# Attention and chunk scores of a hybrid encoder trunk: two heads in step on the two halves of the array

## The chip, the core and the metric

The kernel runs on one core of one Trainium2 chip. The metric is the device time of one execution in microseconds (us). The kernel before takes 2495.84 us, the median of three runs (2495.49 to 2499.09). All products of this kernel run on the tensor engine (PE); VectorE is DVE, ScalarE is ACT, GpSimd is POOL, and SP issues the transfers.

## What is computed

Two layers of an encoder trunk over 512 tokens of 1024 channels, in fp32. Each layer has a half-step feed-forward part, one projection into three mixers that run side by side, an output projection, cross attention to 256 memory tokens, and a second feed-forward part. The change touches two of the mixers, each of six heads of 64 channels:

```python
# B: chunked attention; with 512 tokens every earlier chunk is in the band
s = einsum('bnihd,bnjhd->bhnij', qc, kb) * HEAD_DIM ** -0.5
prob = softmax(where(valid, s + bias, NEG_INF), axis=-1)
o = einsum('bhnij,bnjhd->bnihd', prob, vb)
# A: RWKV-7 recurrence, one step a token
sa = einsum('bhvk,bhk->bhv', S, -kk_t)
S = S * w_t + sa * (kk_t * a_t) + v_t * k_t
y = einsum('bhvk,bhk->bhv', S, r_t)
```

The recurrence is computed by chunks of 64 tokens. Each chunk needs masked products of decayed keys with decayed queries (its scores), the inverse of a triangular system, and a step of the state.

## The kernel before, in words

`trunk` runs `ffn`, `mixer`, `cross`, `ffn` for each layer. Dense products split weights and activations into a high and a low part and multiply three times (`mm3`, L155). All matmuls go through the helper `mm` (L78), elementwise DVE work through `tt` (L69) and `stt` (L72), ACT work through `act` (L75). An fp32 product with fp32 operands shows in the trace as two MATMULs (two passes); a transpose or a product of high and low parts as one.

The change lies in `mixer`, in its second part, where three generators run beside each other. `recurrence` (L618) walks through `systems`, `keyrows` and `chains` and sets the pace: for each of its steps, `dense` (projections of q, k, v and the pool) and `attention` get credit for a fraction of a step (ATT_RATE is 0.65). A `yield` ends a step. On top of that a scheduler orders each engine's instructions when the program is built, so the order on PE is fixed before the run. `dense` makes q and k of two heads a time (`unit`, tiles pqk, pqt); after each of the three units `attend` works on these two heads.

- `attend` (L657) takes the heads of a pair one after the other. A head's q and k lie on one half of the 128 partitions (rows 0 to 63 or 64 to 127). For four blocks of 128 queries: a score product into tile pbs (64 rows of the array, 128, 256, 384 or 512 columns streamed), the bias from tile toe added (tile e, L670), the maximum (L672), the exponential with its sum, a reciprocal (L674), and the scaling (L675). Then ten transposes (pbt, L683), four copies to ptb, and four products with V into tile pbo (64 columns of the array, streams of 512 to 128). Score and transpose tiles share the two PSUM banks "sm". There are 6 heads in each of 2 layers: 48 score products and 48 products with V.
- `systems` (L455) makes the scores of a chunk (tile psc): for head set g of two (row half g of the array), three products of 128 streamed columns, then the masks. Eight chunks a layer, six products each: 96 products.
- `chain` (L530) steps the state: tiles pr, pu, pst, py, with rhs and vu as copies between them, and a group norm at the end of each pair of chunks (pyt).
- After the generators, the output projection (pout, L780 to L790) multiplies first what the attention (mbhi, mblo) and the pool (mchi, mclo) gave, and last what the recurrence gave (mahi, malo).

Tiles ptt and pf are the doubling steps of `systems`, pgate and ppool the gate and the pool, pin, pqk and pbvf dense projections, ptr transposed keys.

Of the kernel before, what the change touches and what calls it, by code (L numbers as in the profile page):

```python
# [8 lines left out]
F32 = mybir.dt.float32  # L9
# [5 lines left out]
P = 128  # L15
T = 512
# [37 lines left out]
def trunk(tc, I, out, depth=DEPTH):  # L54
    nc = tc.nc
    ctx = ExitStack()
    with ctx:
# [73 lines left out]
        ones = const.tile([P, P], F32, name="ones")  # L131
# [42 lines left out]
        def proj_tok_steps(banks, ap, acts):  # L174
            """banks[i][128 tokens, 2, 256] = act[tokens]^T W, for W = ap [128, 8, 256]."""
            w = []
            for k0 in (0, 4):
                w += weights(ap[:, k0:k0 + 4].rearrange("p k m -> p (k m)"), 1024)
                for k in range(k0, k0 + 4):
                    s = slice(k % 2 * 256, k % 2 * 256 + 256)  # L180
                    wh, wl = w[k // 2]
                    ah, al = acts[k]
                    for b, p in enumerate(banks):
                        for i in range(2):
                            c = slice((2 * b + i) * P, (2 * b + i + 1) * P)
                            st = k == 0 and i == 0
                            mm(p[:, i], ah[:, c], wh[:, s], st, False)
                            mm(p[:, i], al[:, c], wh[:, s], False, False)
                            mm(p[:, i], ah[:, c], wl[:, s], False, k == 7 and i == 1)
                    yield  # L190
# [24 lines left out]
        def update(k, p, scale=None, spill=False, fetch=None):  # L215
            """x += scale * p; x leaves for DRAM or is fetched from there around the mixers."""
            if fetch is not None:
                x[k] = fetch
                nc.sync.dma_start(out=x[k], in_=x_dram[k])
            if scale is None:  # L220
                tt(x[k], x[k], p, add)
            else:
                stt(x[k], p, scale, x[k], mult, add)
            if spill:
                nc.sync.dma_start(out=x_dram[k], in_=x[k])
            square_in(k)

        def tok_rstd(sq, n, o, scale, e, tag="sm"):
            """o[128 tokens, n / 128] = 1/sqrt(scale * sum over channels of sq + e)."""
            p = bank(tag, "ptok")  # L230
            for i in range(n // P):
                mm(p[:, i:i + 1], sq[:, i * P:(i + 1) * P], ones[:, 0:1])
            act(o, p[:, :n // P], AF.Sqrt, bias=e, scale=scale)
            nc.vector.reciprocal(out=o, in_=o)

        def rstd(bcast=True, tag="sm"):
            """1/rms of x for each token, with the tokens on the rows and, on request, on the columns."""
            rt = tp.tile([P, 4], F32, tag="rtok", name="rtok", bufs=1)
            tok_rstd(ssq["a"], T, rt, 1.0, eps, tag)
            r = None  # L240
            if bcast:
                p = bank(tag, "psn")
                for i in range(4):
                    mm(p[:, i * P:(i + 1) * P], rt[:, i:i + 1].to_broadcast([P, P]), ident)
                r = tp.tile([P, T], F32, tag="rstd", name="rstd", bufs=1)
                act(r, p, AF.Copy)
            return r, rt
# [46 lines left out]
        def mixer(l):  # L294
# [4 lines left out]
            with mx as mp:  # L299
# [30 lines left out]
                # values  # L330
# [29 lines left out]
                # the low-rank inputs  # L360
# [6 lines left out]
                # while x is in DRAM its eight slots hold scratch of the preparation and then q and k of the attention  # L367
                # (later its output) and the biases
# [65 lines left out]
                # RWKV-7 by chunks of 64, two at a time  # L434
# [20 lines left out]
                def systems(q, o):  # L455
                    """For the pairs 2q and 2q + 1 of chunks, in two sets of heads g, g + 2, g + 4: the masked
                    scores and the inverse of each chunk's triangular system."""
                    nn = mp.tile([P, 2, 3, 2, HD], F32, tag="nn", name="nn", bufs=1)
                    ata, at = [], []
                    for c4 in range(4):  # L460
                        c, c2 = 4 * q + c4, c4 % 2
                        m = mp.tile([P, 3, 2, HD], F32, tag="ata", name="ata", bufs=6)
                        mr = mp.tile([P, 3, 2, HD], F32, tag="atr", name="atr", bufs=6)
                        for g in range(2):
                            s = bank("iv", "psc")[:, :AW].rearrange("p (j t) -> p j t", j=3)
                            for j in range(3):
                                mm(s[:, j], cols(kb, j, c)[halves[g]], cols(ar, j, c)[halves[g]])
                            tt(m[:, :, g], s[:, :, :HD], bc(C("mask")[:, :HD], 3), mult)
                            tt(mr[:, :, g], s[:, :, HD:], bc(C("mask")[:, HD:], 3), mult)
                        u = halves[1 - c2]  # L470
                        act(nn[u, c4 // 2], m[u], AF.Copy)
                        ata.append([m[:, :, g] for g in range(2)])
                        at.append([mr[:, :, g] for g in range(2)])
                        yield
                    # doubling the blocks of b: sources in the even blocks, targets in the odd ones. F holds no more
                    # than its blocks, so that the products need a mask only for which blocks pair up; and until
                    # the last step its 32-blocks hold all of it
# [33 lines left out]
                def keyrows(p):  # L511
                    """Keys on the rows, decayed to the chunk's end."""
# [17 lines left out]
                def chain(p):  # L530
                    """The state through chunks 2p and 2p + 1, and what they put out."""
                    ata, at, F, tr = sys[p]["ata"], sys[p]["at"], sys[p]["F"], trs[p]
                    y = mp.tile([P, 6, HD], F32, tag="y", name="y", bufs=2)
# [42 lines left out]
                    # group norm, bonus, gate  # L576
# [79 lines left out]
                # attention over all earlier chunks and the own one  # L656
                def attend(j, bq, bk, bvt):  # L657
                    po = bank("po", "pbo")
                    for hh in range(2):
                        hr = halves[hh]  # L660
                        toe = toes[hh]
                        nc.sync.dma_start(out=toe, in_=I["toep"][l, 2 * j + hh])
                        nc.gpsimd.memset(toe[0:64, T - HD:], -1e30)
                        prs = []
                        for qi in range(4):
                            n = (qi + 1) * P
                            s = sm("pbs")
                            mm(s[:, :n], bq[hr, qi * P:(qi + 1) * P], bk[hr, :n])
                            e = b2("e")
                            tt(e[:, :n], s[:, :n], toe[:, T - n:], add)  # L670
# [5 lines left out]
                            prs.append(e)  # L676
                            yield
                        pts = []
                        for ki in range(4):
                            n = (4 - ki) * P  # L680
                            pt = sm("pbt")
                            for qi in range(ki, 4):
                                nc.tensor.transpose(pt[:, (qi - ki) * P:(qi - ki + 1) * P], prs[qi][:, ki * P:(ki + 1) * P], ident)  # L683
                            q = mp.tile([P, n], F32, tag=f"ptb{ki}", name="ptb", bufs=1)
                            if ki % 2:
                                nc.vector.tensor_copy(out=q, in_=pt[:, :n])
                            else:
                                act(q, pt[:, :n], AF.Copy)
                            pts.append(q)
                        yield  # L690
                        for ki in range(4):
                            mm(po[hr, ki * P:], bvt[ki][:, (2 * j + hh) * HD:(2 * j + hh + 1) * HD], pts[ki], ki == 0, ki == 3)
# [3 lines left out]
                def pool():  # L696
                    # trailing windows: sums by doubling
                    pwt = mp.tile([P, 2, P], F32, tag="pwt", name="pwt")
                    nc.sync.dma_start(out=pwt, in_=I["poolw"][l])
                    for j in range(2):  # L700
                        def trail(o, i, n):
                            """o = i + i from n tokens before."""
# [58 lines left out]
                # the recurrence sets the pace; the dense products and the attention take steps at these rates beside it  # L761
# [32 lines left out]
        def cross(l):  # L794
            with tc.tile_pool(name=f"cx{l}", bufs=1) as cp:
# [26 lines left out]
                def head(w, acts, n, r, gain, tag, o, b):  # L822
                    """An RMS-normed head; the step it leaves behind puts the channels on the partitions, as high and low parts."""
# [159 lines left out]
def _pack(w, n=P):  # L983
    """[K, M] -> [M / n, 128, K / 128, n]: one contiguous run a partition for each tile of M."""
# [87 lines left out]
```

## Time and profile before

| what | value |
|---|---|
| median of three runs | 2495.84 us (2495.49 to 2499.09) |
| span of the profiled execution, the only time the page gives of it | 2493.6 us, 2.2 us below the median |
| PE busy | 2460.9 us, 99% of the span, 14058 MATMULs |
| DVE, ACT, POOL busy | 1300.3 us, 1007.5 us, 184.9 us |
| granted TensorE clock | 1.00 in every window read |
| second part of the mixer, layer 0 | 478 to 652 us, then the output projection to about 710 |
| the same of layer 1 | 1720 to 1893 us |

The page gives busy time for each engine, the chain of work that ended last, and groups of instructions; the timeline gives starts and lengths. Matmuls are pipelined: the length of one holds its way through the array, so that what a product costs PE is read from the start of one to the start of the next.

### The profile page before, as it was taken

The page shows a single profiled execution, that of the slowest core. Times are in us where ns is not written, and L with a number is a line of the kernel's source. Part 1 is how long each engine was busy: PE and PEld are TensorE (multiplying, and loading weights), DVE is VectorE, ACT ScalarE, POOL GpSimd, SP SyncE. Part 2 cuts the span into 40 slices and gives each one's busy share as a digit, 9 for nine tenths or more (in the row PEclk, how much of TensorE's full clock was granted, in tenths as well). Part 3 has the DMA queues.
Part 4 walks back from the last instruction along what each step waited for, and adds up shares of the span by engine and source line. Part 5 has one row for each costly group of instructions (what it writes and reads, how often), then busy time and mean ns, then how long its engine had stood idle before and what let it go on. Part 6 is the DMA issues. An engine that isn't in the chain of part 4 may idle for free.

```text
span 2493.6 us, 35631 instructions
## 1 busy us (share of the span) xinstructions
PE 2460.9 (99%) x14058; PEld 2001.1 (80%) x14058; DVE 1300.3 (52%) x2361; ACT 1007.5 (40%) x1804; POOL 184.9 (7%) x246
## 2 busy tenths in 40 slices
PE   8999999999999999999999999999999999999999
PEld 6888887877689888888888888867776898888887
DVE  5444335757575644443344443367676756444422
ACT  4333334434465543333333333343344655433322
POOL 1000002101020000000000000021111201000000
PEclk9999999999999999999999999999999999999999
DMA  3223333210242222323332233322102422222332
GB/s 134 95 99 94 106 114 102 69 45 20 68 143 99 71 93 94 102 93 93 93 99 96 95 98 110 119 72 68 45 25 70 148 88 71 94 100 94 99 110 87
DMA packets 72504, 225.27 MB, mean 90 GB/s; under 512 B 8177, under 2 KB 13201, under 8 KB 72337
## 3 DMA queue, kind: packets, MB, share of 16 engines
q1 hardware_dynamic: 72336, 223.00, 27.5%
q8 instruction: 110, 1.80, 0.3%
q14 instruction: 58, 0.47, 0.1%
HBM read 215.89 MB, written 7.08 MB: 89 GB/s over the span
## 4 chain that ended last, share of the span: by engine, by line
PE 95%; DVE 2%; issue 1%; ACT 1%; DMA 1%; POOL 0%; POOLq 0%; ACTq 0%; DVEq 0%; SPq 0%
PE po L78 20%; PE pu L78 20%; PE pg L78 19%; PE pxq L78 5%; PE pin L78 4%; PE pxw L78 3%; PE pqk L78 3%; PE pout L78 3%; PE pxv L78 2%; PE pbs L78 1%; PE pbvf L78 1%; PE pf L78 1%; PE ptt L78 1%; PE pbo L78 1%; PE pr L78 1%; PE psc L78 1%
## 5 line engine op out<-in xcount | busy, mean ns | idle before, releaser
L75 ACT ACTIVATE whi<-raw 128x512 fp32r<-128x512 f32 (+1 forms) x806 | 493.8, 614 | 964.9 <-PE po L78 323.9
L69 DVE TENSOR_TENSOR wlo<-raw,whi 128x512 fp32r<-128x512 f32 (+1 forms) x806 | 550.5, 685 | 570.4 <-ACT whi L75 566.7
L78 PE MATMUL pg<-hhi,whi 128*128 128x512 f32 x704 | 275.4, 391 | 6.6 <-ACT whi L75 6.6
L78 PE MATMUL po<-fhi,whi 128*128 128x512 f32 x704 | 278.1, 395 | 0.0
L78 PE MATMUL po<-fhi,wlo 128*128 128x512 f32 x704 | 278.1, 395 | 0.0
L78 PE MATMUL po<-flo,whi 128*128 128x512 f32 x704 | 278.1, 395 | 0.0
L78 PE MATMUL pg<-hlo,whi 128*128 128x512 f32 x704 | 275.4, 391 | 2.6 <-DVE hlo L72 2.6
L78 PE MATMUL pu<-hhi,wlo 128*128 128x512 f32 x704 | 274.0, 389 | 0.7 <-DVE wlo L69 0.7
L78 PE MATMUL pg<-hhi,wlo 128*128 128x512 f32 x704 | 274.5, 390 | 0.0
L78 PE MATMUL pu<-hhi,whi 128*128 128x512 f32 x704 | 273.9, 389 | 0.0
L78 PE MATMUL pu<-hlo,whi 128*128 128x512 f32 x704 | 273.9, 389 | 0.0
L69 POOL TENSOR_TENSOR ssa<-ssa,sq 128x512 f32<-128x512 f32 x63 | 86.7, 1377 | 1238.4 <-ACT sq L75 1237.8
L78 PEld LDWEIGHTS pg<-hhi,whi 128*128 128x128 f32 x704 | 132.6, 188 | 34.1 <-ACT whi L75 6.6
L78 PEld LDWEIGHTS po<-flo,whi 128*128 128x128 f32 x704 | 131.9, 187 | 32.4
L78 PEld LDWEIGHTS po<-fhi,whi 128*128 128x128 f32 x704 | 131.9, 187 | 32.4
L78 PEld LDWEIGHTS po<-fhi,wlo 128*128 128x128 f32 x704 | 131.9, 187 | 32.2
L78 PEld LDWEIGHTS pg<-hlo,whi 128*128 128x128 f32 x704 | 132.3, 188 | 31.7 <-DVE hlo L72 4.9
L78 PEld LDWEIGHTS pu<-hhi,wlo 128*128 128x128 f32 x704 | 132.1, 188 | 28.4 <-DVE wlo L69 1.2
L78 PEld LDWEIGHTS pg<-hhi,wlo 128*128 128x128 f32 x704 | 132.6, 188 | 27.6 <-DVE wlo L69 0.3
L78 PEld LDWEIGHTS pu<-hhi,whi 128*128 128x128 f32 x704 | 132.1, 188 | 27.7
L78 PEld LDWEIGHTS pu<-hlo,whi 128*128 128x128 f32 x704 | 132.3, 188 | 27.4
L69 DVE TENSOR_TENSOR z<-pg,rstd 128x512 f32<-128x512 f32 x88 | 60.9, 692 | 134.0 <-PE pg L78 124.4
(305 smaller groups left out, 4010.7 us busy)
## 6 DMA issues: line engine op xcount, KB each, us to landing
raw<-in_ffn_wi_dram SPq DMA_DIRECT2D x175, 512.0 KB, 3.5
raw<-in_ffn_wo_dram SPq DMA_DIRECT2D x64, 512.0 KB, 3.5
raw<-in_w_in_dram SPq DMA_DIRECT2D x30, 512.0 KB, 3.5
raw<-in_ffn_wo_dram SPq DMA_DIRECT2D x32, 384.0 KB, 3.1
raw<-in_x_wk_dram SPq DMA_DIRECT2D x16, 512.0 KB, 3.6
raw<-in_x_wv_dram SPq DMA_DIRECT2D x16, 512.0 KB, 3.5
raw<-in_x_wq_dram SPq DMA_DIRECT2D x16, 512.0 KB, 3.5
raw<-in_w_qk_dram SPq DMA_DIRECT2D x12, 512.0 KB, 3.6
```

The costliest lines, as they stand in the source:

```text
L69: (eng or nc.vector).tensor_tensor(out=o, in0=a, in1=b, op=op)
L75: nc.scalar.activation(out=o, in_=i, func=f, **k)
L78: nc.tensor.matmul(o, lhsT=w, rhs=x, start=start, stop=stop)
```

## The change

`attend` takes the two heads of a pair in step. For each query block it issues both score products, one on each row half, each into its own bank; then the DVE and ACT work of both; then, a step later, the transposes of both and one copy a head (ACT for the first head, DVE for the second) into a tile ptb [128, 13, 128] that holds all ten blocks of a head. After the four query blocks the products with V alternate between the heads, that is between column halves. An attention pair has 8 steps where it had 10. Both bias tables are loaded at the pair's start. `systems` issues the scores of a chunk alternating between the head sets, into two banks. Tile y has one buffer for two, `ones` is one column wide for 128, and comments are gone.

```diff
-        ones = const.tile([P, P], F32, name="ones")
+        ones = const.tile([P, 1], F32, name="ones")
...
-                        for g in range(2):
-                            s = bank("iv", "psc")[:, :AW].rearrange("p (j t) -> p j t", j=3)
-                            for j in range(3):
-                                mm(s[:, j], cols(kb, j, c)[halves[g]], cols(ar, j, c)[halves[g]])
+                        sc = [bank("iv", "psc")[:, :AW].rearrange("p (j t) -> p j t", j=3) for _ in range(2)]
+                        for j in range(3):
+                            for g in range(2):
+                                mm(sc[g][:, j], cols(kb, j, c)[halves[g]], cols(ar, j, c)[halves[g]])
+                        for g, s in enumerate(sc):
...
-                    y = mp.tile([P, 6, HD], F32, tag="y", name="y", bufs=2)
+                    y = mp.tile([P, 6, HD], F32, tag="y", name="y", bufs=1)
...
                     po = bank("po", "pbo")
                     for hh in range(2):
-                        hr = halves[hh]
-                        toe = toes[hh]
-                        nc.sync.dma_start(out=toe, in_=I["toep"][l, 2 * j + hh])
-                        nc.gpsimd.memset(toe[0:64, T - HD:], -1e30)
-                        prs = []
-                        for qi in range(4):
-                            n = (qi + 1) * P
-                            s = sm("pbs")
-                            mm(s[:, :n], bq[hr, qi * P:(qi + 1) * P], bk[hr, :n])
+                        nc.sync.dma_start(out=toes[hh], in_=I["toep"][l, 2 * j + hh])
+                        nc.gpsimd.memset(toes[hh][0:64, T - HD:], -1e30)
+
+                    pts = [mp.tile([P, 13, P], F32, tag="ptb", name="ptb", bufs=2) for _ in range(2)]
+                    for qi in range(4):
+                        n = (qi + 1) * P
+                        ss = [sm("pbs") for _ in range(2)]
+                        for hh, hr in enumerate(halves):
+                            mm(ss[hh][:, :n], bq[hr, qi * P:(qi + 1) * P], bk[hr, :n])
+                        es = []
+                        for hh in range(2):
                             e = b2("e")
-                            tt(e[:, :n], s[:, :n], toe[:, T - n:], add)
+                            tt(e[:, :n], ss[hh][:, :n], toes[hh][:, T - n:], add)
...
-                            prs.append(e)
-                            yield
-                        pts = []
-                        for ki in range(4):
-                            n = (4 - ki) * P
+                            es.append(e)
+                        yield
+                        for hh in range(2):
                             pt = sm("pbt")
-                            for qi in range(ki, 4):
-                                nc.tensor.transpose(pt[:, (qi - ki) * P:(qi - ki + 1) * P], prs[qi][:, ki * P:(ki + 1) * P], ident)
-                            q = mp.tile([P, n], F32, tag=f"ptb{ki}", name="ptb", bufs=1)
-                            if ki % 2:
-                                nc.vector.tensor_copy(out=q, in_=pt[:, :n])
+                            for ki in range(qi + 1):
+                                nc.tensor.transpose(pt[:, ki * P:(ki + 1) * P], es[hh][:, ki * P:(ki + 1) * P], ident)
+                            o = pts[hh][:, qi:4 * qi + 1:3]
+                            i = pt[:, :n].rearrange("p (k t) -> p k t", t=P)
+                            if hh:
+                                nc.vector.tensor_copy(out=o, in_=i)
                             else:
-                                act(q, pt[:, :n], AF.Copy)
-                            pts.append(q)
-                        yield
-                        for ki in range(4):
-                            mm(po[hr, ki * P:], bvt[ki][:, (2 * j + hh) * HD:(2 * j + hh + 1) * HD], pts[ki], ki == 0, ki == 3)
+                                act(o, i, AF.Copy)
+                        yield
+                    for ki in range(4):
+                        for hh, hr in enumerate(halves):
+                            mm(po[hr, ki * P:], bvt[ki][:, (2 * j + hh) * HD:(2 * j + hh + 1) * HD],
+                               pts[hh][:, 4 * ki:3 * ki + 4].rearrange("p k t -> p (k t)"), ki == 0, ki == 3)
```

As built, the two score products of a query block stand side by side on PE in 22 of 24 cases; the 512-wide block of each layer's first pair has other rows between. The two products with V stand side by side in 22 of 24 cases; the 512-wide ones of each layer's third pair have a product py between. Of the scores of the recurrence, the first chunk of a layer stands in three pieces of two products, one of each head set, before and now; the second, third, fourth, sixth and eighth stand in one piece of six, before and now; the fifth stands in pieces of 3, 2 and 1 products where it had 1, 2 and 3, the seventh in two pieces of three, before and now.

The thinnest place between score products and their transposes is in the last pair of heads, layer 0, on PE. Before, where a row of pbs is one head's:

```order
L78 MATMUL pbs<-xs_3019,xs_3018 128x256
L78 MATMUL ptt<-G,nn 64x64 x12
L78 MATMUL pgate<-a_3010,lora 128x128 x3
L78 MATMUL pf<-F,tm 64x64 x12
L78 MATMUL pin<-hhi,whi 128x512
L78 MATMUL pin<-hlo,whi 128x512
L78 MATMUL pin<-hhi,wlo 128x512
```

and now:

```order
L78 MATMUL pbs<-xs_3019,xs_3018 128x256 x2
L78 MATMUL ptt<-G,nn 64x64 x12
L78 MATMUL pgate<-a_3010,lora 128x128 x3
L78 MATMUL pin<-hhi,whi 128x512
L78 MATMUL pin<-hlo,whi 128x512
L78 MATMUL pin<-hhi,wlo 128x512
L78 MATMUL pf<-F,tm 64x64 x12
L78 MATMUL pin<-hhi,whi 128x512
L78 MATMUL pin<-hlo,whi 128x512
L78 MATMUL pin<-hhi,wlo 128x512
L685 MATMUL pbt<-cst,e 128x128 x4
```

Both heads' scores stand in one row, and nine rows later the transposes of both, which before stood at the end of each head.

The end of the attention of layer 0, on PE, from its last products with V. Before:

```order
L78 MATMUL pbo<-ptb,bvt 64x256
L78 MATMUL pbo<-ptb,bvt 64x128
L78 MATMUL pst<-vu_2941,tr 64x64 x6
L78 MATMUL ppool<-pl,pwt 128x512
L78 MATMUL py<-vu_2941,atr 64x64 x2
L78 MATMUL py<-state_3423,ar 64x128
L78 MATMUL py<-vu_2941,atr 64x64 x2
L78 MATMUL py<-state_3423,ar 64x128
L78 MATMUL py<-vu_2941,atr 64x64 x2
L78 MATMUL py<-state_3423,ar 64x128
L78 MATMUL pout<-mbhi,whi 128x512 x2
```

and now:

```order
L78 MATMUL pbo<-ptb,bvt 64x128 x2
L78 MATMUL py<-state_3425,ar 64x128
L78 MATMUL py<-vu_2940,atr 64x64 x2
L78 MATMUL py<-state_3425,ar 64x128
L78 MATMUL py<-vu_2940,atr 64x64 x2
L78 MATMUL py<-state_3425,ar 64x128
L78 MATMUL pr<-vu_2941,ata 64x64 x6
L78 MATMUL pr<-state_3423,ar 64x128 x3
L78 MATMUL ppool<-pl,pwt 128x512
L78 MATMUL pu<-rhs,F 64x64 x6
L78 MATMUL pst<-vu_2941,tr 64x64 x6
L78 MATMUL pout<-mbhi,whi 128x512 x2
```

The attention ends earlier against the recurrence, so that pr, pu and pst of the next chunk now lie between its end and the first row of pout; pu and pst stand next to each other.

The last rows of the output projection that don't need the recurrence, on PE, layer 0. Before:

```order
L78 MATMUL pout<-mbhi,wlo 128x512
L593 MATMUL pyt<-cst,y 128x128 x3
L78 MATMUL pout<-mchi,whi 128x512
L78 MATMUL pout<-mclo,whi 128x512
L78 MATMUL pout<-mchi,wlo 128x512
L78 MATMUL pout<-mchi,whi 128x512
L78 MATMUL pout<-mclo,whi 128x512
L78 MATMUL pout<-mchi,wlo 128x512
L78 MATMUL pout<-mahi,whi 128x512 x3
```

and now:

```order
L78 MATMUL pout<-mchi,whi 128x512
L78 MATMUL pout<-mclo,whi 128x512
L78 MATMUL pout<-mchi,wlo 128x512
L594 MATMUL pyt<-cst,y 128x128 x3
L78 MATMUL pout<-mahi,whi 128x512 x3
```

Six products that stood between the transposes of the recurrence's output and the first product that needs it now stand ahead of them.

## Rows read from the trace of the kernel before

**Rows 1.** Page, part 1: busy time, share, instructions of each engine.
```profile
PE 2460.9 (99%) x14058; PEld 2001.1 (80%) x14058; DVE 1300.3 (52%) x2361; ACT 1007.5 (40%) x1804; POOL 184.9 (7%) x246
```
**Rows 2.** Page, part 4: the chain that ended last, by engine.
```profile
PE 95%; DVE 2%; issue 1%; ACT 1%; DMA 1%; POOL 0%; POOLq 0%; ACTq 0%; DVEq 0%; SPq 0%
```
**Rows 3.** Busy time in two windows of layer 0: length, then each engine.
```profile
478.00:652.00 174.00, 171.83 (x1930) 131.04 (x1928) 115.50 (x316) 68.48 (x139) 24.40 (x52) 1.00 0.11 36
652.00:695.00 43.00, 40.86 (x240) 30.44 (x241) 28.01 (x60) 21.92 (x48) 7.78 (x8) 1.00 0.34 106
```
**Rows 4.** Waits of PE, whole trace: us in total, times, longest.
```profile
PE pout L78 <- ACT mbhi L75: 3.5, 2, 1.8
...
PE pout L78 <- ACT mahi L75: 2.1, 3, 1.0
```
**Rows 5.** Timeline of PE, row halves, scores of chunks: start, length, count of passes.
```profile
447.96 0.49 PE L78 MATMUL psc<-ar,kb 64*128 64x128 f32 x4
448.38 0.50 PE L78 MATMUL pbvf<-hhi,whi 128*128 128x512 f32 x1
...
478.19 1.26 PE L78 MATMUL psc<-ar,kb 64*128 64x128 f32 x12
...
550.24 1.58 PE L78 MATMUL psc<-ar,kb 64*128 64x128 f32 x12
551.75 0.57 PE L78 MATMUL pst<-vu,tr 128*64 128x64 f32 x12
552.25 0.93 PE L78 MATMUL psc<-ar,kb 64*128 64x128 f32 x6
```
**Rows 6.** Timeline of PE, the four score products of one head.
```profile
502.19 0.48 PE L78 MATMUL pbs<-xs,xs 64*128 64x128 f32 x2
...
507.54 0.70 PE L78 MATMUL pbs<-xs,xs 64*128 64x256 f32 x2
...
510.64 0.91 PE L78 MATMUL pbs<-xs,xs 64*128 64x384 f32 x2
...
516.43 1.12 PE L78 MATMUL pbs<-xs,xs 64*128 64x512 f32 x2
```
**Rows 7.** Timeline of PE, column halves: eight alternating products, then a head's products with V.
```profile
422.11 1.09 PE L78 MATMUL pkinv<-cst,kst 128*64 128x128 f32 x16 [1.29 <-DVE kst L406]
423.13 0.50 PE L78 MATMUL pin<-hhi,wlo 128*128 128x512 f32 x1
...
523.59 2.37 PE L78 MATMUL pbo<-ptb,bvt 128*64 128x512 f32 x8
525.88 0.49 PE L78 MATMUL pbs<-xs,xs 64*128 64x128 f32 x2
```
**Rows 8.** Timeline of PE: two neighbours in the output projection.
```profile
654.04 0.40 PE L78 MATMUL pout<-mbhi,whi 128*128 128x512 f32 x1
654.27 0.39 PE L78 MATMUL pout<-mblo,whi 128*128 128x512 f32 x1
```
**Rows 9.** Groups of DVE, 478 to 652 us: count, busy us, mean ns, idle before.
```profile
L551 DVE COPY vu<-pu 64x384 f32<-64x384 f32 x6 | 3.3, 545 | 2.6 <-PE pu L78 2.6
...
L69 DVE TENSOR_TENSOR e<-pbs,xs 128x256 f32<-128x256 f32 x6 | 2.5, 423 | 3.8 <-PE pbs L78 3.7
L672 DVE TENSOR_REDUCE bst<-e 128x1 f32<-128x256 f32 x6 | 2.4, 408 | 0.1
L675 DVE TENSOR_SCALAR e<-e,bst 128x256 f32<-128x256 f32 x6 | 2.1, 349 | 0.1
```
**Rows 10.** Groups of ACT in the same stretch.
```profile
L75 ACT ACTIVATE e<-e,bst 128x256 f32<-128x256 f32 x6 | 3.0, 507 | 2.9 <-DVE bst L672 2.8
...
L75 ACT ACTIVATE ptb<-pbt 128x256 f32<-128x256 f32 x6 | 2.3, 380 | 2.7 <-PE pbt L683 2.7
```
**Rows 11.** Instructions on tile pbo: weight loads, ns min/median/max.
```profile
L78 PEld LDWEIGHTS pbo<-ptb,bvt x96: 133/137/137, 523.6 to 1889.3; 128*64 128x64 f32 x96
```

More of the change, by code (lines that the diff above doesn't have):

```diff
@@ L231, in tok_rstd @@
             for i in range(n // P):
-                mm(p[:, i:i + 1], sq[:, i * P:(i + 1) * P], ones[:, 0:1])
+                mm(p[:, i:i + 1], sq[:, i * P:(i + 1) * P], ones)
             act(o, p[:, :n // P], AF.Sqrt, bias=e, scale=scale)
```

## The prediction
> **What bounds the kernel now.** I read the page's busy times first: PE is busy for 99% of the span, DVE for 52%, ACT for 40% [rows 1]. A busy PE alone proves little, since the lengths of pipelined products overlap; so the chain that ended last comes second, and 95% of it is PE [rows 2]. Third, the part that changes: in the 174 us of layer 0 from 478 us on, PE is busy for 171.8, DVE for 115.5 (66%), ACT for 68.5, at the full granted clock, 1.00; in the 43 us after it PE has about 2 us of gaps [rows 3]. Fourth, what PE waits for: in and after this part the largest are the two waits of the output projection for mbhi, the attention's output split (3.5 us over both layers), then for mahi, the recurrence's (2.1) [rows 4]. So here a microsecond less of array time is a microsecond less, as long as producers keep up.
>
> **How array time is read.** The cost of a product is from its start to the next start; the printed length reaches 0.07 us further: four passes psc start at 447.96, are printed with 0.49, and the next product starts at 448.38, after 0.42 [rows 5]. I take 0.07 off throughout.
>
> **Does alternating halves help? Before has both cases.** Row halves: that run of four passes is two products on different halves, and takes 0.42. Three products of one half in a row (six passes) take 0.93 - 0.07 = 0.86, six take 551.75 - 550.24 = 1.51, and six that the scheduler happened to mix 1.19 [rows 5]. A lone product on a half takes 0.41 (128 columns, as first of a head) [rows 6]. So an alternating pair costs what one product costs, to 0.01 us, and a further product or pair in the same run costs (0.86 - 0.42) / 2 = 0.22. Column halves: sixteen passes pkinv of 128 columns, alternating, take 1.02; a head's products with V, not alternating, stream 2 x 1280 columns in 525.88 - 523.59 = 2.29, some 0.11 a 128-column pass, so that sixteen in file would be 1.76 [rows 7]. Alternating halves overlap in both directions, also with two different streams: six products pst take 0.50 [rows 5]. Not shown is a pair of 512 columns; I take the same rule for it.
>
> **The sum, array time.**
> - Scores of attention: one head costs 0.41 + 0.63 + 0.84 + 1.05 = 2.93 [rows 6], twelve heads 35.2. Six pairs at 2.93 + 0.06 are 17.9; the order leaves one 512 block a layer unpaired, 2 x 1.04 more. Change: **-15.2 us**.
> - Products with V: twelve heads at 2.29 are 27.5 [rows 7]; six pairs at 2.35 are 14.1; one 512-wide pair a layer is torn apart, 2 x 0.95. Change: **-11.5 us**.
> - Scores of the recurrence, per layer: the first of eight chunks stands in alternating pairs already. The next three have six in a row, 1.19 each, now three pairs in a run, 0.42 + 2 x 0.22 = 0.86: -0.99. Of the last four, two have 1.51 each and become 0.86: -1.30. One in two pieces of three has 2 x 0.86, now a pair and a single each, 2 x 0.64: -0.44. One in pieces of 1, 2 and 3 (0.42 + 0.64 + 0.86) becomes 0.64 + 0.42 + 0.42: -0.44 [rows 5]. Both layers: **-6.3 us**.
> - Transposes, copies, masks: the same number of the same sizes; DVE copies 1280 columns a pair for 1024, ACT 1280 for 1536. The narrower `ones` is one memset, y with one buffer is written by the next pair of chunks steps after it was read. Bias tables: the same transfers, both at a pair's start. All 0, covered by PE's queue of dense products; without that cover the copies would enter the waits below. Ends of this line: -1.5 to +1.5.
>
> Array time: -33.0 us.
>
> **The sum, waits.**
> - In the new order pr, ppool, pu and pst stand ahead of the first mbhi product, over 3 us of work against a longest wait of 1.8: the 3.5 us go. **-3.5** (ends -3.5 and 0) [rows 4].
> - The six products that stood behind pyt are gone from there, 6 x 0.23 of cover a layer, so PE stands that much longer for mahi: **+2.7** (0 to +2.7) [rows 8].
> - pu and pst of one chunk stand side by side with the copy to vu between them, 0.545 us: **+1.3** with its start, in two layers (0 to +1.5) [rows 9].
> - Attention steps: each of the 24 query blocks now makes PE's transposes wait for the exponentials of both heads, and the next scores for both copies, since scores and transposes use the same two banks. Queued behind a waiting transpose on PE are dense products and the recurrence's steps. For a 256-wide block the chain is 0.42 + 0.41 + 0.51 + 0.35 = 1.7 us for the first head and 1.2 of DVE more for the second, 2.9 [rows 9, 10]. The thinnest place of the order holds, between the two, two runs of twelve 64x64 products (six of that kind take 0.50, so about 1.0 each, an estimate), three pgate (like three scores, 0.86) and six dense products at 0.23: 4.2. So most steps are covered. Lower end 0; upper end 0.7 a step, as if PE stood through a copy (0.38) and its starts each time: 17. I take 0.1 a step, near the lower end, since the cover exceeds the chain: **+2.4** (0 to +17).
>
> Waits: +2.9. Together **-30.1**: the profiled span 2493.6 becomes 2463.5. The median stands 2.2 above that span, so I predict **2466 us** for the median, 1.2% less.
>
> **The rivals.**
> - *Producers become the pace.* DVE's 115.5 us in a stretch that shrinks by some 16 are 73% of it instead of 66%; a queue that full may be late at many steps. At the upper end of 0.7 a step the time is 2466 + 15 = 2481. Against it: DVE's idle time is spread over its groups, and ACT has over half its time free. For it: the Trainium skill, "TensorEngine Tiling (Array Packing)", PSUM Bottleneck, says that tiling speeds up the matmuls and leaves the emptying of PSUM as it was, which may then become the bottleneck. The trace of before can't show that state.
> - *Column halves don't overlap at these lengths,* because the weight loads of the two heads come in file. A load takes 0.137 us [rows 11]; 96 of them in the open are 13 us, about the 11.5 forecast for the products with V: 2466 + 11.5 = 2477.5. The Trainium skill, "TensorE: Matmul & The Clock Gate", The mechanism, says that a weight load overlaps running products only where the row group differs; column halves share their rows, so by that rule the gain on V is lost. Against it: pkinv and pst are column halves and do overlap [rows 5, 7], and eight loads (1.1 us) would not fit into 2.29 us beside the 2.2 of streaming if they were in the open now. Low chance.
> - *The pair of banks makes attention a chain (slower).* If the transposes always met an empty queue, PE would stand 2.9 us a step, 24 x 2.9 = 70, and the time is 2495.8 - 30 + 70 = 2535. It decides from 33 / 24 = 1.4 us a step on. Against it: the cover counted above at the thinnest place.
> - *No concurrency at 512 columns, or pairs torn.* Then only the recurrence's scores gain, and the steps cost a little: about 2491.
>
> **How the numbers follow.** The forecast (PE stays the bound, waits small) gets 0.72; producers 0.15; column halves 0.08; no concurrency 0.02; the chain of banks 0.03. Low end: array time -34.5 and waits -3.5, that is 2495.8 - 38 = 2458, and 2 for the noise: 2456. High end: takes in column halves (2477.5) and most of the producers' case: 2481. What is left out is some of that case, the slow rival and the torn one, under 0.15. A difference under 0.2% (5 us, about what a measurement of this kernel tells from none) holds only if gains and waits happen to cancel. Faster 0.93, same 0.04, slower 0.03.
>
> **What would show it.** In the new trace: four passes pbs of 512 columns in about 1.07 us from first to next start; sixteen passes pbo in about 2.35; twelve psc in 0.86 where six stand in a row. PE's waits for mbhi gone, for mahi near 3 us a layer. The mixer's second part some 15 us shorter a layer, DVE near 73% there. Wrong it would be if pairs show two streams one after the other, or if waits of PE for e, ptb or the pbs banks add up to over 10 us; then the gain is there and eaten.

## The result, and the profile after

The changed kernel takes **2477.49 us** (median of 4 runs, 2476.63 to 2477.89); the kernel before, beside it, 2497.37 (4 runs, 2495.49 to 2499.09). The ratio is 0.9919 [0.9905, 0.9933]: 19.9 us less, where the sum said 30.1. Forecast was 2466 in a range of 2456 to 2481.

The page after, busy times and the chain that ended last, beside [rows 1, 2]:

```profile
PE 2439.1 (99%) x14058; PEld 1996.1 (81%) x14058; DVE 1297.3 (52%) x2361; ACT 1000.2 (40%) x1800; POOL 189.9 (8%) x246
...
PE 94%; DVE 3%; issue 1%; DMA 1%; ACT 1%; POOL 0%; POOLq 0%; DVEq 0%; ACTq 0%; SPq 0%
```

PE is still the bound, with fewer microseconds of work. The two windows of layer 0 that answer to [rows 3], each with the length, then busy time of PE, weight loads, DVE, ACT and POOL, clock, DMA share and GB/s:

```profile
481.00:642.00 161.00, 157.62 (x1917) 125.65 (x1917) 114.35 (x316) 65.22 (x137) 25.04 (x51) 1.00 0.12 39
642.00:690.00 48.00, 43.73 (x263) 32.78 (x262) 30.92 (x63) 23.40 (x51) 11.88 (x12) 1.00 0.32 96
```

The second part is 13 us shorter (161 for 174), DVE is at 71% in it, and PE's gaps rose from 2.2 to 3.4 us. In the stretch after it they rose from 2.1 to 4.3.

To see where the gain arose, take the mixer as a whole, from its first product psc to the first product of cross attention. It shrank from 262.24 to 252.30 us in layer 0 and from 262.83 to 251.20 in layer 1: -21.6 together. PE's groups of the edited tiles over the mixer of layer 0 (count, busy us, mean ns, idle before), before:

```profile
L78 PE MATMUL pbs<-xs,xs 64*128 64x128 f32 (+3 forms) x48 | 19.0, 479 | 0.0
L78 PE MATMUL pbo<-ptb,bvt 128*64 128x512 f32 (+3 forms) x48 | 14.8, 442 | 0.0
L78 PE MATMUL psc<-ar,kb 64*128 64x128 f32 x96 | 12.4, 294 | 0.0
```

and after:

```profile
L78 PE MATMUL pbs<-xs,xs 64*128 64x128 f32 (+3 forms) x48 | 12.3, 482 | 0.0
L78 PE MATMUL psc<-ar,kb 64*128 64x128 f32 x96 | 11.1, 296 | 0.0
L78 PE MATMUL pbo<-ptb,bvt 128*64 128x512 f32 (+3 forms) x48 | 8.6, 439 | 0.0
```

The same instructions, each as long as before, in fewer microseconds: they lie beside each other. Busy time holds the tail of a product, so the table adds instead, as the prediction did, from each start on PE to the next, for each tile over the mixer (us per layer, both layers alike):

```
tile                       before   after    change   forecast
pbs (scores)                17.41   11.35    -6.05    -7.6
pbo (products with V)       13.66    7.73    -5.94    -5.75
psc (recurrence's scores)   11.51   10.19    -1.32    -3.15
py<-state (mbhi wait)        7.14    6.23    -0.91    -1.75
pyt to mahi                  1.47    3.45    +1.98    +1.35
pu                           6.71    7.36    +0.65    +0.65
```

Outside the mixers this execution is some 4.1 us longer than that of before, at places that the change doesn't touch: 2.8 us before the first mixer, where the first 50 us have a mean granted clock of 0.97 for 1.00, and 1.4 us after the last, where the granted clock is 0.51 from 1945.7 to 1949.2 us. So the spans differ by only 17.5 us, 2493.6 to 2476.1.

PE's waits after. The wait for mbhi [rows 4] is gone; that for mahi has grown:

```profile
PE pout L78 <- ACT mahi L75: 3.9, 2, 2.0
...
PE ptt L78 <- DVE G L491: 1.8, 2, 0.9
PE pr L78 <- ACT y L75: 1.8, 2, 0.9
...
PE pst L78 <- DVE vu L552: 1.3, 2, 0.6
...
PE pout L78 <- ACT whi L75: 1.0, 1, 1.0
PE pyt L594 <- DVE y L69: 1.0, 2, 0.5
...
PE pout L78 <- DVE wlo L69: 0.8, 1, 0.8
```

### The profile page after: what moved, and what is told of

It reads as the page before. It is cut to its first block, busy times and chain, and to the rows that moved or that the text cites. A ratio compares the mean times of both kernels' runs of the same rounds, so it can differ in the third digit from the quotient of the medians.

```text
span 2476.1 us, 35629 instructions
## 1 busy us (share of the span) xinstructions
PE 2439.1 (99%) x14058; PEld 1996.1 (81%) x14058; DVE 1297.3 (52%) x2361; ACT 1000.2 (40%) x1800; POOL 189.9 (8%) x246
## 4 chain that ended last, share of the span: by engine, by line
PE 94%; DVE 3%; issue 1%; DMA 1%; ACT 1%; POOL 0%; POOLq 0%; DVEq 0%; ACTq 0%; SPq 0%
PE po L78 20%; PE pu L78 20%; PE pg L78 19%; PE pxq L78 5%; PE pin L78 5%; PE pout L78 3%; PE pxw L78 3%; PE pqk L78 3%; PE pxv L78 2%; PE pbvf L78 1%; PE pf L78 1%; PE ptt L78 1%; PE pr L78 1%; PE pxs L78 1%; PE pxo L78 1%; DVE wlo L69 1%
```

## The experiments

The first theory: halves of the array overlap, and that is the gain; the shortfall is in scores of chunks that don't alternate, attention pairs whose second product is late, and the bare tail. Its rival: the gain comes from the schedule, since an attention pair has 8 steps for 10 and the end of the mixer is ordered anew. Ratios are to the kernel before on the same chip (2498.86 or 2498.96 us there), so that a kernel is compared with the change by its ratio and by the length of its mixers, not by bare times.

**1. Only the recurrence's scores alternate.** The kernel before with this edit alone:

```diff
-                        for g in range(2):
-                            s = bank("iv", "psc")[:, :AW].rearrange("p (j t) -> p j t", j=3)
-                            for j in range(3):
-                                mm(s[:, j], cols(kb, j, c)[halves[g]], cols(ar, j, c)[halves[g]])
+                        sc = [bank("iv", "psc")[:, :AW].rearrange("p (j t) -> p j t", j=3) for _ in range(2)]
+                        for j in range(3):
+                            for g in range(2):
+                                mm(sc[g][:, j], cols(kb, j, c)[halves[g]], cols(ar, j, c)[halves[g]])
+                        for g, s in enumerate(sc):
```

> The kernel before with the alternating scores of the recurrence alone. Theory O (array time of pairs that run together is the gain): the trace of the changed kernel shows 1.3 us a layer less for tile psc, so 2 to 4 us under before (about 2494). Theory S (the gain is in the attention's order of steps and fewer waits, the overlap is hidden): no change, within 1 us of before.

Measured: 2496.78 us, ratio 0.9990 [0.9982, 0.9999]. In the trace psc falls by 1.32 and 1.34 us a layer and the mixers by as much. This term is worth 2.6 us, not 6.3. The timeline of the changed kernel tells why (start, length, count of passes):

```profile
480.99 0.94 PE L78 MATMUL psc<-ar,kb 64*128 64x128 f32 x12
481.86 0.39 PE L78 MATMUL pqk<-whi,hhi 128*128 128x256 f32 x1
...
549.81 1.58 PE L78 MATMUL psc<-ar,kb 64*128 64x128 f32 x12
551.32 0.57 PE L78 MATMUL pst<-vu,tr 128*64 128x64 f32 x12
```

The first run of six takes 0.87, as three pairs should; the later one 1.51, as before [rows 5]. As built, with the buffers' numbers shown, the order on PE is for these two runs:

```
psc_3632  psc_3633  psc_3632  psc_3633  psc_3632  psc_3633
...
psc_4566 x3  psc_4567 x3
```

The scheduler, free to reorder, put the last three chunks three and three by head set; they cost what they did before. The rows without numbers read "x6" for both.

**2. The products with V a head at a time,** all else as changed:

```diff
-                    for ki in range(4):
-                        for hh, hr in enumerate(halves):
+                    for hh, hr in enumerate(halves):
+                        for ki in range(4):
```

> The changed kernel, but the products with V of a pair in file, first head then second, all else in step. Theory O: tile pbo goes from 7.7 back to about 13.7 us a layer, so 11 to 12 us over the changed kernel (about 2489). Theory S: within 2 us of the changed kernel (2477.5), since steps, copies and scores are as there.

Measured: 2483.08 us, ratio 0.9932 [0.9920, 0.9944]; the mixers are 4.9 and 3.6 us longer than with the change, pbo 3.2 a layer; the rest of layer 0 is the output projection (+1.7), which has a granted clock of 0.50 from 674.9 to 681.7 us. So the alternation is worth something by itself, though only 6.4 of the 11.9 us that this term gained. The timeline shows the reason; two heads in file:

```profile
577.40 3.93 PE L78 MATMUL pbo<-ptb,bvt 128*64 128x512 f32 x16
581.26 0.50 PE L78 MATMUL pin<-hhi,whi 128*128 128x512 f32 x1
```

3.86 us, not 2 x 2.29 = 4.58: the second head's first 512-column pass starts 6 ns after the first pass of the first head's third product, ahead of what stands between them in the order. Products on different halves overlap at the seam even where the program has them in file.

**3. The scores of attention a head at a time,** with a step after each head and the rate raised in proportion to the steps (0.65 x 12 / 8), so that attention ends at the same place of the recurrence:

```diff
-LEAD, DENSE_RATE, ATT_RATE = 15, (1.0, 0.61, 0.98), 0.65
+LEAD, DENSE_RATE, ATT_RATE = 15, (1.0, 0.61, 0.98), 0.975
...
-                        ss = [sm("pbs") for _ in range(2)]
-                        for hh, hr in enumerate(halves):
-                            mm(ss[hh][:, :n], bq[hr, qi * P:(qi + 1) * P], bk[hr, :n])
                         es = []
-                        for hh in range(2):
+                        for hh, hr in enumerate(halves):
+                            s = sm("pbs")
+                            mm(s[:, :n], bq[hr, qi * P:(qi + 1) * P], bk[hr, :n])
...
-                        yield
+                            yield
```

> The changed kernel, but a step lies between the score products of the two heads of a block (12 steps a pair, rate 0.975 for 0.65, so that the attention keeps its pace); products with V and the recurrence's scores alternate as there. Theory O: at most 2 of 24 score pairs still stand together, tile pbs goes from 11.4 to about 16.5 us a layer, so 9 to 11 us over the changed kernel (about 2487). Theory S: within 2 us of it.

Measured: 2491.56 us, ratio 0.9969 [0.9959, 0.9979]; the mixers are 6.9 and 8.3 us longer than with the change, pbs 4.7 a layer. Its group of pbs over the mixer of layer 0 is back near that of before, and PE waits for the exponentials:

```profile
L78 PE MATMUL pbs<-xs,xs 64*128 64x128 f32 (+3 forms) x48 | 18.3, 479 | 0.0
...
PE pbt L684 <- DVE e L678: 4.6, 6, 1.5
```

The overlap of the scores is the larger part of the loss, though four of the 24 pairs still stand together in the order as built. The rest is such waits, pgate (+1.7 a layer) and, in layer 1, the output projection (+1.3). So this run doesn't measure the overlap alone; the rival's claim, that the time would stay near the change's, is out by 6.9 and 8.3 us of mixer.

**4. The scores of a chunk held in alternation.** `mm` now returns its instruction, and each product is issued after the one before:

```diff
+                        last = None
                         for j in range(3):
-                            for g in range(2):
-                                mm(sc[g][:, j], cols(kb, j, c)[halves[g]], cols(ar, j, c)[halves[g]])
+                            for g in (1, 0):
+                                with (tc.issue_after(last.ins) if last is not None else nullcontext()):
+                                    last = mm(sc[g][:, j], cols(kb, j, c)[halves[g]], cols(ar, j, c)[halves[g]])
```

> The changed kernel with the order of a chunk's six score products fixed, second head set first, so that chunks six to eight alternate on PE too (built, they stand three and three by head set in the changed kernel). Theory O with the shortfall on psc put down to that order: psc falls by 1.8 us a layer, 2 to 4 us under the changed kernel (about 2474). Rival: the second head set's bank comes late, so alternating only moves the wait onto PE: no gain or 1 to 3 us slower.

Measured: 2472.29 us, ratio 0.9891 [0.9878, 0.9904]. psc falls from 10.19 to 9.35 a layer, the mixers by 2.3 and 0.6. Better, but less than half of the 1.8 expected, and not the 8.36 that the forecast's pairs give: the seventh chunk, two runs of 0.86 in the changed kernel, now reads

```profile
552.31 0.48 PE L78 MATMUL psc<-ar,kb 64*128 64x128 f32 x2
552.72 0.33 PE L687 MATMUL pbt<-cst,e 128*128 128x128 f32 x1
552.98 0.93 PE L78 MATMUL psc<-ar,kb 64*128 64x128 f32 x10
```

The first product starts, the second 0.67 us later, then they alternate. PE doesn't wait between them: in the order as built a transpose stands there, and in the sixth and eighth chunk three products pqk and three pr. The edit fixes the order of the six among themselves, not that they stand side by side, so that the first costs 0.42 alone and the chunk 1.28 instead of 0.86. Why the scheduler put other products there is not settled.

**5. Attention slower against the recurrence.** The rate had been set for 10 steps a pair; 8 steps take 0.52 for 0.65:

```diff
-LEAD, DENSE_RATE, ATT_RATE = 15, (1.0, 0.61, 0.98), 0.65
+LEAD, DENSE_RATE, ATT_RATE = 15, (1.0, 0.61, 0.98), 0.52
```

> The changed kernel with the attention's step rate 0.52 for 0.65 (8 steps a pair where there were 10, so its pace against the recurrence is as before the change). Theory: the step rate left as it was let the attention end early, which tore pairs and uncovered the recurrence's end; in the new order the 512-wide scores of the first pair stand together (-1.0 us a layer), the fifth and seventh chunk alternate (-1 us a layer), and six products stand again behind the last pyt (-1.4 us a layer): 4 to 8 us under the changed kernel (about 2471). Rival: the waits only move to other places: within 2 us of 2477.5.

Measured: 2472.17 us, ratio 0.9891 [0.9879, 0.9904]. Over the mixer pbs is 9.84 us a layer for 11.35, a change of -7.57 against before; psc 8.72 for 10.19, with not a line of it edited; the step from pyt to mahi 1.47 for 3.45, as before. In turn the wait for mbhi is back and transposes wait:

```profile
PE pout L78 <- ACT mbhi L75: 2.5, 2, 1.2
PE py L78 <- DVE state L69: 2.4, 2, 1.2
PE pout L78 <- ACT mahi L75: 2.1, 3, 0.9
...
PE pbt L685 <- DVE e L679: 1.8, 4, 0.6
```

The 512-wide pairs say where the rest came from. One of the changed kernel, on PE:

```profile
566.57 1.84 PE L78 MATMUL pbs<-xs,xs 64*128 64x512 f32 x4
568.33 0.45 PE L78 MATMUL py<-vu,atr 128*64 128x64 f32 x4
```

and on DVE at the same time, the second head's copy out of the transposes' bank:

```profile
566.67 0.55 DVE L689 COPY ptb<-pbt 128x384 f32<-128x384 f32 x1
```

The pair takes 1.76; its second product starts 0.72 after the first, some 0.05 after the copy's end. So it does in all four late pairs of the changed kernel. Scores and transposes share the two banks "sm": the first head's bank was emptied by ACT in time, the second's not. With the rate at 0.52, PE and then DVE:

```profile
529.99 1.13 PE L78 MATMUL pbs<-xs,xs 64*128 64x512 f32 x4
531.05 0.62 PE L78 MATMUL pf<-F,tm 64*64 64x64 f32 x14
```

```profile
528.94 0.56 DVE L689 COPY ptb<-pbt 128x384 f32<-128x384 f32 x1 [1.02 <-PE pbt L685]
```

Here the copy ends at 529.50, before the pair, and the pair takes 1.06, where a single 512-column product takes 1.05 [rows 6]. Of the three such pairs a layer the changed kernel has one torn and two late by 0.72; at the rate of 0.52 one is on time, one late by 0.14 and one by 0.72.

**6 to 8. Mends together.** Run 6 (forced052) is the edits of runs 4 and 5 in one kernel. Run 7 (allforced052) is run 6 with the pairs of attention held in alternation too:

```diff
-                        for hh, hr in enumerate(halves):
-                            mm(ss[hh][:, :n], bq[hr, qi * P:(qi + 1) * P], bk[hr, :n])
+                        last = None
+                        for hh in (1, 0):
+                            hr = halves[hh]
+                            with (tc.issue_after(last.ins) if last is not None else nullcontext()):
+                                last = mm(ss[hh][:, :n], bq[hr, qi * P:(qi + 1) * P], bk[hr, :n])
```

and the same for the products with V. Run 8 (forced050) is run 6 with

```diff
-LEAD, DENSE_RATE, ATT_RATE = 15, (1.0, 0.61, 0.98), 0.52
+LEAD, DENSE_RATE, ATT_RATE = 15, (1.0, 0.61, 0.98), 0.5
```

> The changed kernel with both mends, the fixed order of the recurrence's scores and the attention's rate 0.52. If the two losses are different ones, the gains add up less what the rate alone already gave back on chunks five and seven: 2 to 4 us under either alone, about 2469. If both only removed the same waits: 2472.

> As the one before, and the order is fixed too in the score pairs and in the products with V, second head first, so that the product whose bank or copy comes late goes first and both start together. Theory of the late partner (the second head's 512-wide scores start 0.7 us late for want of a bank, its first product with V for want of its copy): tile pbs near 9.0 and pbo near 7.1 us a layer, 1 to 3 us under the one before. Rival: the wait only moves ahead of the pair, and torn pairs and the shorter cover of the last pyt cost: 0 to 3 us over it.

> As forced052 with rate 0.50. The order leaves all products with V in pairs and seven products behind the last pyt, but tears a 384-wide and a 256-wide score pair a layer (+1.4 us a layer). Theory O: within 3 us of forced052, either way; a difference of over 4 us would need a cause other than pairs.

Measured: 2471.64, 2472.25 and 2475.37 us, ratios 0.9891 [0.9878, 0.9905], 0.9899 [0.9883, 0.9915] and 0.9904 [0.9889, 0.9919]. The gains don't add. In run 6 psc is 8.33 a layer, near the forecast's value, though by other chunks, but pbo rose from 7.73 to 8.96, and its mixers (250.3 and 250.9) are no shorter than those of run 5 (249.9 and 250.5). In run 7 pbo is 7.14, as expected, but pbs 11.12 instead of 9.0, with the 128- and 256-wide pairs of the third pair of heads torn, and pyt to mahi 3.68. In run 8 the mixers are 251.9 and 252.0, and the time is 3.7 us over run 6, outside the 3 expected; its trace has 3.2 us of waits of the output projection for weights, and in both layers a granted clock of 0.50 for 6.8 us at the end of the attention. In runs 4 to 7 the mixers take 250 to 251 us: what one mend gave, other places took back.

Runs 4, 5 and 6 can't be told apart. Each is about 7 us under the changed kernel by the ratios and 5 by the medians, of which the mixers show 2.9, 3.1 and 2.4; the rest lies in stretches that no edit touches, so only the smaller figure is shown to be theirs. Of run 4's 2.9, psc is 1.7.

## Why the prediction was right or wrong

**The bound and the direction: right.** PE's time was the bound, and overlapping halves took array time away. Runs 2 and 3 each undo one overlap, keep the rest, and lose 6.4 us of pbo and 9.4 of pbs again. The size was not right: 19.9 us for 30.1. The time lies in the range through the room at its upper end, which was made for two rivals that didn't come true, and in that it was lucky.

**Scores of attention, -15.2 forecast, -12.1 measured.** The rule for a pair held, at 512 columns too (1.06). What the term missed is that a pair costs one product only if its two banks are free together. The sentence "the next scores for both copies, since scores and transposes use the same two banks" named this dependence, but priced it as a wait that dense products cover. It is not covered there: the first head's product has started, and the second waits for DVE's copy. Two pairs a layer late by 0.72 are 2.9 of the 3.1 us missing. Run 5, with one such pair a layer and none torn, gives -15.1.

**Products with V, -11.5 forecast, -11.9 measured.** The sum is right, its parts are not. The first two pairs of layer 0 after:

```profile
538.88 3.15 PE L78 MATMUL pbo<-ptb,bvt 128*64 128x512 f32 x16
...
577.78 2.50 PE L78 MATMUL pbo<-ptb,bvt 128*64 128x512 f32 x16
580.21 0.50 PE L78 MATMUL pin<-hhi,whi 128*128 128x512 f32 x1
```

The second takes 2.43, near the 2.35 of a pair. The first takes 3.08 (the next product starts at 541.96). Its second head starts 0.78 late, at 539.66, because that head's copy is late again; DVE:

```profile
538.92 0.69 DVE L689 COPY ptb<-pbt 128x512 f32<-128x512 f32 x1 [1.49 <-PE pbt L685]
```

And the torn pair, with py beside it, cost no 0.95 more: 7.73 - 3.08 - 2.43 leaves 2.22 for it. That the term came out is therefore in part luck.

**Scores of the recurrence, -6.3 forecast, -2.65 measured.** The step that failed is "Of the last four, two have 1.51 each and become 0.86", with the seventh chunk's pair and single beside it: of this 1.74 a layer nothing came, while the second to fifth chunk gave 1.32 of 1.43. I took the loop of the source, alternating, for the order on PE. The rows of the order that I read had no buffer numbers and could not show it; with numbers, the sixth to eighth chunks stand three and three. A pair itself costs what I said (0.87 at 480.99). The runs of 1.19 before were not mixed by the scheduler either, as the prediction has it: with numbers, they stand three and three too (psc_3632 x3, psc_3638 x3 at 478.19).

**Waits, +2.9 forecast, +5.5 in the list.** PE's waits in the two mixers rose from 8.0 to 13.5 us. Three of the four terms came as said. The wait for mbhi went, -3.5; py shows only -1.8 of it, since a new wait for y, ahead of pr, stands behind the same product (0.9 a layer). pu and pst side by side cost 1.3. The end of the recurrence cost what was said, +2.7: before, in layer 0, from the product ahead of the last pyt,

```profile
678.94 0.39 PE L78 MATMUL pout<-mbhi,wlo 128*128 128x512 f32 x1
...
682.29 0.97 PE L78 MATMUL pout<-mahi,whi 128*128 128x512 f32 x3 [0.95 <-ACT mahi L75]
```

and after

```profile
670.14 0.39 PE L78 MATMUL pout<-mchi,wlo 128*128 128x512 f32 x1
...
673.50 0.96 PE L78 MATMUL pout<-mahi,whi 128*128 128x512 f32 x3 [1.96 <-ACT mahi L75]
```

It is 3.35 us before and 3.36 after, though six products less stand in it, 6 x 0.23 = 1.4 a layer. The +1.98 of pyt in the table is larger because the wait of before stood behind the pool's products and not behind pyt. Of the attention steps, +2.4, the transposes were covered: no wait for e is in the list. The copies were not, as above, and a late second product doesn't show in a list of waits, since PE is busy with the first.

**What the sum had not at all** are waits at other places, some 5 us: for y ahead of pr 1.8, for weights of the output projection 1.8, in layer 0 alone, and for G and tm in `systems` 1.5 more than before. A shorter chain of array work moves every step against the producers; that this is what made these waits is argued, not tested.

**Rivals.** *Producers become the pace:* the time lies near its 2481, but not for its reason: DVE is at 71% and far from full; it is late at a few places. The lateness of 0.7 that it wanted at all 24 steps came at four of them. The Trainium skill, "TensorEngine Tiling (Array Packing)", PSUM Bottleneck, says that the emptying of PSUM may become the bottleneck; the trace agrees at the pairs that wait for a copy of 0.55 to 0.69 us, and not for the kernel, where PE is still 94% of the chain. *Column halves don't overlap* would have given 2477.5, the time measured, and is wrong all the same: in run 6 two heads' products with V take

```profile
598.08 2.37 PE L78 MATMUL pbo<-ptb,bvt 128*64 128x512 f32 x16
600.38 0.49 PE L78 MATMUL pbs<-xs,xs 64*128 64x128 f32 x4
```

2.30 us, what one head takes [rows 7]. By the rule of the Trainium skill, "TensorE: Matmul & The Clock Gate", The mechanism, that a weight load overlaps running products only where the row group differs, the sixteen loads of 0.137 (2.2 us) would have stood in the open; the measurement decides against it for these halves. The same section of the Trainium skill also lets a load into a background weight buffer be pulled ahead of running products; no run here tells whether that is what happens. *A chain of banks* and *no concurrency* are out by their times, 2535 and 2491. A time that fits a rival is no proof of it: only the terms by tile told these apart.

## What to carry to other kernels

Two independent streams on different halves of the array, rows or columns, cost about what one costs, if they stand in alternation in the order as built and both destinations are free: empty both banks early, read that order with its buffer numbers, and read each pair's time from its start to the next start. A change that shortens or regroups a generator's steps needs its step rate set anew; here that was worth as much as forcing the order, and the two did not add. Leave cover between a serial end (here the group norm) and its user: the longer wait there, 2 us, was followed by a lower clock in seven of ten cases here.

## What I had not expected of the hardware

**A product on the idle half starts ahead of products queued before it for the busy half.** The order of before at the end of the attention is pbo 256 columns, pbo 128, then pst (printed above). The timeline of before has

```profile
647.08 0.43 PE L78 MATMUL pbo<-ptb,bvt 128*64 128x256 f32 x1
647.09 0.33 PE L78 MATMUL pst<-vu,tr 128*64 128x64 f32 x2
647.34 0.49 PE L78 MATMUL pbo<-ptb,bvt 128*64 128x256 f32 x2
647.56 0.27 PE L78 MATMUL pst<-vu,tr 128*64 128x64 f32 x1
647.67 0.27 PE L78 MATMUL pbo<-ptb,bvt 128*64 128x128 f32 x1
```

pst starts 10 ns after the first pass of the 256-column product, ahead of the 128-column one. Run 2 showed the same with whole heads. So part of the overlap was there before the change, where the order put two halves near each other. It also shows in psc: six products, three and three, took 1.19 in some places and 1.51 in others [rows 5], and the second head set's first pass starts 0.33 us after the run's start in the first (478.19) and 0.65 in the second (550.24). What lets it start early in one place and not in the other is not shown.

**A gap in PE's work was followed by a lower clock.** At the end of layer 1, after (start, length, wait before):

```profile
1902.76 0.52 PE L594 MATMUL pyt<-cst,y 128*128 128x128 f32 x3 [0.49 <-DVE y L69]
1905.24 1.65 PE L78 MATMUL pout<-mahi,whi 128*128 128x512 f32 x3 [1.96 <-ACT mahi L75]
1906.68 0.63 PE L78 MATMUL pout<-malo,whi 128*128 128x512 f32 x1
1907.11 0.63 PE L78 MATMUL pout<-mahi,wlo 128*128 128x512 f32 x1
...
1908.51 0.39 PE L78 MATMUL pout<-mahi,wlo 128*128 128x512 f32 x1
1908.74 0.40 PE L78 MATMUL pout<-mahi,whi 128*128 128x512 f32 x1
```

and the window of the stretch behind the waits:

```profile
1904.70:1908.20 3.50, 2.96 (x7) 2.41 (x8) 2.68 (x7) 2.75 (x7) 0.00 (x0) 0.51 0.81 241
```

Neighbours are 0.43 apart and then 0.23 again [rows 8]; the granted clock was 0.51, the level of 1.2 GHz for 2.4. The nine products from mahi on take 3.50 us there (1905.24 to 1908.74) and 2.65 in layer 0 of the same run (from 673.50 on), so that some 0.8 us came on top of the two waits. Layer 0, with waits of the same size, had no such stretch (clock 1.00 from 642 to 690 us). Runs 2, 4 and 7, with the same waits, had it in both layers, and run 3, with the same waits too, in neither: seven cases of ten. Before and runs 5 and 6, where the wait for mahi is about 1 us, had it in neither. So such a gap doesn't decide it alone, and what else does is not shown. What the clock costs there is part of what a bare tail costs.
